# Later flips and value products in the first attention of a two-block transformer kernel

## The chip, the cores and the metric

One core of a Trainium2 chip runs the whole kernel in one launch. The metric is the device time of one execution in microseconds (us), as the median of several runs. Five engines with queues of their own work side by side: TensorE (PE, matmuls), VectorE (DVE), ScalarE (ACT), GpSimd (POOL) and SyncE (SP, which here issues the transfers).

## The reference

Two blocks run one after the other on 256 tokens with 2048 channels, all in float32. The change touches only the first stage, the attention of the first block:

```python
h = rms_norm(x, mixer_norm)                       # x is (1, 256, 2048)
q, k, v = split(h @ w_qkv)                        # 32 query heads, 4 key and value heads of 64
q, k = apply_rope(rms_norm(q, q_norm)), apply_rope(rms_norm(k, k_norm))
scores = q @ k.T / 8                              # in a band of 128 keys back; blocks of 128 queries
m = max(max(scores), sink)
probs = exp(scores - m) / (sum(exp(scores - m)) + exp(sink - m))
x = x + (probs @ v) @ w_o
```

The 32 query heads fall into 4 groups of 8, one for each key head. Behind this attention come a gated feed-forward, a mixer with a gated linear attention and a pooling branch, a cross attention and a second feed-forward, which the change leaves as they are.

## The kernel before, in words

**The large products.** Every projection is a product of activations (2 tiles `t` of 128 tokens) with a weight matrix that streams from memory in units of 512 rows by 512 columns. A unit is four k-tiles of 128 rows. To keep float32 accuracy, each number is split into a high and a low part, and a k-tile takes three matmuls for each `t` (`mm`, L280 to L282), six in all, into two PSUM banks tagged `acc`. The weights are split into `wh` (on ACT, L235) and `wl` (on DVE, L236), two k-tiles at a time and three such parts ahead.

**The first attention.** `attention` runs five chunks of 16 k-tiles through `gemm`: first the keys and values (k-tiles 0 to 15), then the query groups g = 0 to 3 (k-tiles 16 to 31, 32 to 47, 48 to 63, 64 to 79). Then the output projection `w_o` follows (from k-tile 80). In this text the k-tiles are numbered so, and "at k-tile n" means behind the six matmuls of k-tile n.

**Jobs.** What must be done with a finished chunk is a Python generator, a job. `gemm` calls `tick` after each k-tile, which counts every job's wait down by one; a job whose count is 0 writes its next instructions into the program, up to its next `yield n`, and comes up again n k-tiles later. TensorE takes its instructions in exactly the order in which the program writes them. The instructions of DVE, ACT and POOL are put in order by a scheduler that may move them; each of these engines then also works its list off in order. `norm_rope` writes its instructions with a raised priority. Where a later stage needs the output of a job that isn't finished, `need` runs the rest of the job at once.

**`kv_job`** starts 4 k-tiles after its chunk. It scales the values, normalises and rotates the keys (`norm_rope`: L611 on ACT, L613, L614, the power L445 on POOL, then L619, L621, L625, L627 and L630 on DVE), waits, and flips the keys with TensorE transposes (L663), one `t` per k-tile.

**`attn_job(g)`** starts when the chunk of its group is done. Group 0 rotates both `t` in one step, the other groups the first at once and the second 2 k-tiles later. Then, with waits between: flips of the queries (L681, four transposes for each `t`, copied by ACT L682), the scores of `t` = 0 (L695, 16 matmuls), the first half of the scores of `t` = 1 (8 matmuls), the flips of the probabilities of `t` = 0 (L725, twice four, copied by ACT L727), the second half of the scores of `t` = 1, the value products of `t` = 0 (L734, 16 matmuls into the one bank tagged `po`), the four flips of `t` = 1 with the value products of the flip before in the same k-tile (8 matmuls each), and two k-tiles later the flips of the output (L421), which become activations for `w_o`. Behind the scores, DVE adds the mask while it empties the bank (L700), takes the maximum (L702, L703), and ACT takes the exponentials (L708). L739 on DVE empties `po`, and the next value products wait for it. All small products of the jobs take turns in three PSUM banks tagged `aux`, and the temporaries in 12 buffers tagged `s2`.

The jobs of neighbouring groups overlap: that of group g is in its second half while the chunk of group g + 1 ends and that group's rotations begin.

Of the kernel before, what the change touches and what calls it, by code (L numbers as in the profile page):

```python
# [83 lines left out]
class _Net:  # L84
# [563 lines left out]
    def kv_job(self, kv):  # L648
        nc = self.nc
        yield 4  # L650
        self.need(self.start)
        v = self.s2([128, 2, 256])
        kd = [self.s2([128, 4, 2, 64]) for _ in range(2)]
        for t in range(2):
            nc.scalar.activation(v[:, t], kv[t][:, 256:512], AF.Identity, bias=0.0, scale=self.r[:, t:t + 1])
        self.norm_rope([z[:, 0:256].rearrange("p (h d) -> p h d", d=64) for z in kv], 4, (0, 1),
                       self.rope[1], 1.0, [[z[:, :, j] for j in range(2)] for z in kd])
        yield 9
        kT = self.s4([128, 4, 256])
        for t in range(2):  # L660
            b = self.bank((128, 4, 128))
            for h in range(4):
                nc.tensor.transpose(b[:, h], kd[t][:, h], self.ident)  # L663
            nc.scalar.copy(kT[:, :, t * 128:t * 128 + 128], b)
            yield 1
        return kT, v

    def attn_job(self, g, qs):

        nc = self.nc  # L670
        q = [self.s2([128, 4, 2, 64]) for _ in range(2)]
        for ts in ((0, 1),) if g == 0 else ((0,), (1,)):
            self.norm_rope([qs[t].rearrange("p (h d) -> p h d", d=64) for t in ts], 8, ts, self.rope[0], 0.125,
                           [[q[t][:, :, i] for i in range(2)] for t in ts], split=True)
            yield 7 if g == 0 else 4 if ts[0] else 3
        kT, v = self.need(self.kv)
        qT = self.s4([128, 4, 256])
        for t in range(2):
            b = self.bank((128, 4, 128))
            for j in range(4):  # L680
                nc.tensor.transpose(b[:, j], q[t][:, j], self.ident)  # L681
            nc.scalar.copy(qT[:, :, t * 128:t * 128 + 128], b)  # L682
            yield 2
        nm = [self.sm([128, 8]) for _ in range(2)]
        den = [self.sm([128, 8]) for _ in range(2)]

        def scores(t, u):

            nb, hp, res = t + 1, 4 // (t + 1), []
            mask = self.mask2 if t else self.mask1  # L690
            bs = [self.bank((128, hp, nb * 128)) for _ in range(2)]
            for i in range(hp):
                for half, b in enumerate(bs):
                    rows = slice(64 * half, 64 * half + 64)
                    nc.tensor.matmul(b[:, i], qT[rows, u + i, t * 128:t * 128 + 128],  # L695
                                     kT[rows, g, 0:nb * 128], start=True, stop=True)
            for half, b in enumerate(bs):
                h0 = 4 * half + u
                s = self.s2([128, hp, nb * 128])
                nc.vector.tensor_tensor(s, b, mask.unsqueeze(1).to_broadcast([128, hp, nb * 128]), op=ALU.add)  # L700
                mx = self.sm([128, hp])
                nc.vector.tensor_reduce(mx, s, axis=AX.X, op=ALU.max)  # L702
                nc.vector.scalar_tensor_tensor(nm[t][:, h0:h0 + hp], mx, -1.0,  # L703
                                               self.nsink[:, 8 * g + h0:8 * g + h0 + hp],
                                               op0=ALU.mult, op1=ALU.min)
                for i in range(hp):
                    h = h0 + i
                    nc.scalar.activation(s[:, i], s[:, i], AF.Exp, bias=nm[t][:, h:h + 1],  # L708
                                         accum_out=den[t][:, h:h + 1])
                res.append((h0, s))  # L710
            return res

        def totals(t):
            es = self.sm([128, 8])
            nc.vector.tensor_add(es, nm[t], self.sink[:, 8 * g:8 * g + 8])
            nc.scalar.activation(es, es, AF.Exp)
            nc.vector.tensor_add(den[t], den[t], es)
            nc.vector.reciprocal(den[t], den[t])

        def flipped(t, s):  # L720
            nb, hp = t + 1, 4 // (t + 1)
            b = self.bank((128, hp, nb, 128))
            for i in range(hp):
                for j in range(nb):
                    nc.tensor.transpose(b[:, i, j], s[:, i, j * 128:j * 128 + 128], self.ident)  # L725
            pt = self.s2([128, hp, nb, 128])
            nc.scalar.copy(pt, b)  # L727
            return pt

        def weighted(po, t, h0, pt):  # L730
            nb, hp = t + 1, 4 // (t + 1)
            for i in range(hp):
                for j in range(nb):
                    nc.tensor.matmul(po[:, h0 + i], pt[:, i, j], v[:, j, g * 64:g * 64 + 64],  # L734
                                     start=j == 0, stop=j == nb - 1)

        def rows(po, t):
            o = self.s2([128, 512])
            nc.vector.tensor_tensor(o.rearrange("p (h d) -> p h d", d=64), po,  # L739
                                    den[t].unsqueeze(2).to_broadcast([128, 8, 64]), op=ALU.mult)  # L740
            return o

        s0 = scores(0, 0)
        totals(0)
        yield 2
        s1 = scores(1, 0)
        yield 2
        p0 = [(h0, flipped(0, s0[0][1])) for h0 in (s0[0][0],)]
        yield 1
        p0.append((s0[1][0], flipped(0, s0[1][1])))  # L750
        yield 1
        s1 += scores(1, 2)
        totals(1)
        yield 1
        po = self.bank((128, 8, 64), "po")
        for h0, pt in p0:
            weighted(po, 0, h0, pt)
        o = [rows(po, 0)]
        yield 1
        po, prev = None, None  # L760
        for h0, s in s1:
            pt = flipped(1, s)
            yield 1
            if prev is not None:
                if po is None:
                    po = self.bank((128, 8, 64), "po")
                weighted(po, 1, *prev)
            prev = (h0, pt)
        yield 1
        weighted(po, 1, *prev)  # L770
        o.append(rows(po, 1))
        hl = yield from self.group_job(o, wait=2)
        return hl
# [558 lines left out]
```

## Time and profile before

| | |
|---|---|
| runs | 2686.42, 2686.44, 2686.57 us (median 2686.44) |
| profiled execution, its own time | 2686.66 us |
| its span, first to last instruction | 2684.5 us |
| PE busy | 2657.9 us (99%) |
| PEld (weight loads) busy | 2195.2 us (82%) |
| DVE busy | 1890.7 us (70%) |
| ACT busy | 1424.2 us (53%) |
| POOL busy | 27.1 us (1%) |
| DMA share of 16 engines | 51.4% |
| granted TensorE clock | 0.999 |

Busy is the union of an engine's instructions. A matmul of 512 columns is listed with 0.39 us, though the next one starts 0.23 us after it: they overlap, so a busy TensorE can still lose time. Idle time in the tables is that of the engine just before an instruction, with what ended it.

### The profile page before, as it was taken

The page shows a single profiled execution, that of the slowest core. Times are in us where ns is not written, and L with a number is a line of the kernel's source. Part 1 is how long each engine was busy: PE and PEld are TensorE (multiplying, and loading weights), DVE is VectorE, ACT ScalarE, POOL GpSimd, SP SyncE. Part 2 cuts the span into 40 slices and gives each one's busy share as a digit, 9 for nine tenths or more (in the row PEclk, how much of TensorE's full clock was granted, in tenths as well). Part 3 has the DMA queues.
Part 4 walks back from the last instruction along what each step waited for, and adds up shares of the span by engine and source line. Part 5 has one row for each costly group of instructions (what it writes and reads, how often), then busy time and mean ns, then how long its engine had stood idle before and what let it go on. Part 6 is the DMA issues. An engine that isn't in the chain of part 4 may idle for free.

```text
span 2684.5 us, 31592 instructions
## 1 busy us (share of the span) xinstructions
PE 2657.9 (99%) x12352; PEld 2195.2 (82%) x12352; DVE 1890.7 (70%) x2225; ACT 1424.2 (53%) x1849; POOL 27.1 (1%) x27
## 2 busy tenths in 40 slices
PE   8999999999999999999999999999999999999998
PEld 7778888888888888888888888888878888888887
DVE  7775799888888864655545555454578877777776
ACT  6555555555555555454444555444555655555554
POOL 0100000000000000000000000000000000000000
PEclk9999999999999999999999999999999999999999
DMA  7334455555555554445555566444554555555553
GB/s 304 113 126 145 169 218 187 205 192 206 209 195 200 194 187 178 151 172 188 188 190 193 183 225 212 172 157 168 183 180 175 190 193 194 192 190 195 194 193 138
DMA packets 74086, 499.61 MB, mean 186 GB/s; under 512 B 8496, under 2 KB 9392, under 8 KB 14928
## 3 DMA queue, kind: packets, MB, share of 16 engines
q1 hardware_dynamic: 73936, 497.59, 51.4%
q8 instruction: 97, 1.59, 0.2%
q14 instruction: 53, 0.43, 0.0%
HBM read 495.46 MB, written 2.10 MB: 185 GB/s over the span
## 4 chain that ended last, share of the span: by engine, by line
PE 97%; DVE 2%; ACT 1%; POOL 0%; DMA 0%; issue 0%; SPq 0%; POOLq 0%; DVEq 0%; ACTq 0%
PE acc L280 29%; PE acc L282 29%; PE acc L281 29%; PE aux L421 2%; PE aux L282 1%; PE aux L281 1%; PE aux L280 1%; PE po L734 1%; PE po L282 1%; PE po L281 1%; PE po L280 1%; PE aux L969 0%; POOL sm L445 0%; DVE wl L236 0%; DMA raw<-in_w_qkv 0%; PE aux L695 0%
## 5 line engine op out<-in xcount | busy, mean ns | idle before, releaser
L236 DVE TENSOR_TENSOR wl<-raw,wh 128x1024 fp32r<-128x1024 f32 (+1 forms) x1012 | 1230.7, 1220 | 689.0 <-ACT wh L235 677.1
L235 ACT CAST wh<-raw 128x1024 fp32r<-128x1024 f32 (+1 forms) x1012 | 1060.2, 1051 | 1084.0 <-PE acc L282 1020.6
L280 PE MATMUL acc<-wh,s 128*128 128x512 f32 x3440 | 1364.1, 397 | 7.4 <-ACT wh L235 5.5
L282 PE MATMUL acc<-wh,s 128*128 128x512 f32 x3440 | 1342.6, 390 | 0.6 <-DVE s L404 0.6
L281 PE MATMUL acc<-wl,s 128*128 128x512 f32 x3440 | 1341.0, 390 | 0.4 <-DVE wl L236 0.4
L280 PEld LDWEIGHTS acc<-wh,s 128*128 128x128 f32 x3440 | 646.9, 188 | 145.5 <-DVE s L382 7.1
L282 PEld LDWEIGHTS acc<-wh,s 128*128 128x128 f32 x3440 | 646.2, 188 | 138.1 <-DVE s L404 1.1
L281 PEld LDWEIGHTS acc<-wl,s 128*128 128x128 f32 x3440 | 647.3, 188 | 128.2 <-DVE wl L236 1.7
L467 DVE TENSOR_TENSOR x<-acc,x 128x512 f32<-128x512 f32 x112 | 72.8, 682 | 0.0
L421 PEld LDWEIGHTS aux<-con,s 128*128 128x128 f32 x408 | 50.2, 140 | 15.7 <-issue 4.0
L421 PE MATMUL aux<-con,s 128*128 128x128 f32 x408 | 60.9, 272 | 1.8 <-DVE s L1162 1.8
L1159 ACT ACTIVATE s<-aux,vec 128x256 f32<-128x256 f32 x88 | 47.9, 560 | 12.5 <-PE aux L421 7.8
L403 ACT CAST s<-aux 128x512 fp32r<-128x512 f32 x66 | 38.4, 584 | 28.9 <-PE aux L421 18.6
L445 POOL TENSOR_TENSOR sm<-sm,mhalf 128x2 f32<-128x2 f32 (+3 forms) x22 | 26.0, 1182 | 2651.0 <-DVE sm L453 2314.1
L404 DVE TENSOR_TENSOR s<-aux,s 128x512 fp32r<-128x512 f32 x66 | 44.6, 687 | 11.5 <-ACT s L403 10.3
L408 ACT ACTIVATE s<-aux,vec 128x256 fp32r<-128x256 f32 x80 | 37.7, 473 | 22.3 <-PE aux L421 14.2
L280 PE MATMUL aux<-wh,s 128*128 128x512 f32 x120 | 46.7, 389 | 0.0
L281 PE MATMUL aux<-wl,s 128*128 128x512 f32 x120 | 46.7, 389 | 0.0
L282 PE MATMUL aux<-wh,s 128*128 128x512 f32 x120 | 46.7, 389 | 0.0
L409 DVE SCALAR_TENSOR_TENSOR s<-aux,vec,s 128x256 fp32r<-128x256 f32 x80 | 38.3, 482 | 6.5 <-ACT s L408 5.3
L1160 DVE SCALAR_TENSOR_TENSOR s<-aux,vec,s 128x255 f32<-128x255 f32 x88 | 41.0, 478 | 2.4 <-ACT s L1159 0.2
L1162 DVE SCALAR_TENSOR_TENSOR s<-aux,vec,s 128x254 f32<-128x254 f32 x88 | 40.0, 477 | 1.1
(195 smaller groups left out, 1309.1 us busy)
## 6 DMA issues: line engine op xcount, KB each, us to landing
raw<-in_w_up SPq DMA_DIRECT2D x132, 1024.0 KB, 4.8
raw<-in_w_dn SPq DMA_DIRECT2D x88, 1024.0 KB, 4.8
raw<-in_w_in SPq DMA_DIRECT2D x64, 1024.0 KB, 4.8
raw<-in_w_gate SPq DMA_DIRECT2D x44, 1024.0 KB, 4.8
raw<-in_w_ckv SPq DMA_DIRECT2D x32, 1024.0 KB, 4.7
raw<-in_w_qkv SPq DMA_DIRECT2D x19, 1024.0 KB, 5.4
raw<-in_w_o SPq DMA_DIRECT2D x16, 1024.0 KB, 4.7
raw<-in_w_br SPq DMA_DIRECT2D x16, 1024.0 KB, 4.7
```

Of the source, the lines that this page charges most:

```text
L235: nc.scalar.copy(h[:, m], raw[:, m])
L236: nc.vector.tensor_sub(l[:, m], raw[:, m], h[:, m].bitcast(F32))
L280: nc.tensor.matmul(o, ah[:, k, s], h, start=first, stop=False)
L281: nc.tensor.matmul(o, ah[:, k, s], l, start=False, stop=False)
L282: nc.tensor.matmul(o, al[:, k, s], h, start=False, stop=last)
L403: nc.scalar.copy(h[:, k0:k0 + n], src)
L404: nc.vector.tensor_sub(l[:, k0:k0 + n], src, h[:, k0:k0 + n].bitcast(F32))
L421: self.nc.tensor.transpose(b[:, j, t * 128:t * 128 + 128], srcs[t][:, (k + j) * 128:(k + j) * 128 + 128], self.ident)
L467: nc.vector.tensor_add(xs[t], pss[t], xs[t])
L1159: nc.scalar.activation(y[:, j], b[:, j], AF.Identity, bias=bb, scale=w2)
L1160: nc.vector.scalar_tensor_tensor(y[:, j, 1:256], b[:, j, 0:255], w1, y[:, j, 1:256], op0=ALU.mult, op1=ALU.add)
L1162: nc.vector.scalar_tensor_tensor(y[:, j, 2:256], b[:, j, 0:254], w0, y[:, j, 2:256], op0=ALU.mult, op1=ALU.add)
```

## The change

Five waits of the jobs become longer; no instruction is added or taken away. The keys are flipped 10 k-tiles after their rotation was written instead of 9. In group 0 the first query flips come 9 k-tiles after the rotation instead of 7. In groups 0 to 2 the first flip of the probabilities of `t` = 0 comes 3 k-tiles after the scores instead of 2, and the value products of `t` = 0 come 2 k-tiles after the second half of the scores of `t` = 1 instead of 1. All that a job does behind a longer wait moves with it; group 3 keeps its waits.

```diff
@@ kv_job
                        self.rope[1], 1.0, [[z[:, :, j] for j in range(2)] for z in kd])
-        yield 9
+        yield 10
         kT = self.s4([128, 4, 256])
@@ attn_job
             self.norm_rope([qs[t].rearrange("p (h d) -> p h d", d=64) for t in ts], 8, ts, self.rope[0], 0.125,
                            [[q[t][:, :, i] for i in range(2)] for t in ts], split=True)
-            yield 7 if g == 0 else 4 if ts[0] else 3
+            yield 9 if g == 0 else 4 if ts[0] else 3
         kT, v = self.need(self.kv)
...
         s1 = scores(1, 0)
-        yield 2
+        yield 3 if g < 3 else 2
         p0 = [(h0, flipped(0, s0[0][1])) for h0 in (s0[0][0],)]
         yield 1
         p0.append((s0[1][0], flipped(0, s0[1][1])))
         yield 1
         s1 += scores(1, 2)
         totals(1)
-        yield 1
+        yield 2 if g < 3 else 1
         po = self.bank((128, 8, 64), "po")
```

The places in k-tiles, before and after, worked out from the waits:

| | group 0 | group 1 | group 2 |
|---|---|---|---|
| rotations written | 31 (both) | 47 and 49 | 63 and 65 |
| query flips | 37, 39 → 39, 41 | 53, 55 | 69, 71 |
| scores of t = 0, first half of t = 1 | 41, 43 → 43, 45 | 57, 59 | 73, 75 |
| flips of t = 0 | 45, 46 → 48, 49 | 61, 62 → 62, 63 | 77, 78 → 78, 79 |
| second half of the scores of t = 1 | 47 → 50 | 63 → 64 | 79 → 80 |
| value products of t = 0 | 48 → 52 | 64 → 66 | 80 → 82 |
| flips of t = 1 | 49 to 52 → 53 to 56 | 65 to 68 → 67 to 70 | 81 to 84 → 83 to 86 |
| value products of t = 1 | 51 to 54 → 55 to 58 | 67 to 70 → 69 to 72 | 83 to 86 → 85 to 88 |
| output flips | 56, 57 → 60, 61 | 72, 73 → 74, 75 | 88, 89 → 90, 91 |

Group 3 rotates at 79 and 81, flips its queries at 85 and 87, and goes on as the groups before it did. The flips of the keys move from k-tiles 27 and 28 to 28 and 29.

## Rows read from the trace of the kernel before

**Rows 1.** The page's section 1, all engines: busy us (share) xinstructions.
```profile
PE 2657.9 (99%) x12352; PEld 2195.2 (82%) x12352; DVE 1890.7 (70%) x2225; ACT 1424.2 (53%) x1849; POOL 27.1 (1%) x27
```

**Rows 2.** The page's section 5, high part of the weights: | busy, mean ns | idle before, releaser.
```profile
L235 ACT CAST wh<-raw 128x1024 fp32r<-128x1024 f32 (+1 forms) x1012 | 1060.2, 1051 | 1084.0 <-PE acc L282 1020.6
```

**Rows 3.** Waits of PE, whole span: waited for, total us, times, longest.
```profile
PE aux L725 <- DVE s L700: 3.5, 3, 1.4
PE aux L681 <- DVE s L630: 2.8, 2, 1.6
...
PE po L734 <- DVE sm L703: 1.4, 3, 0.5
```

**Rows 4.** Timeline of PE, group 0's query flips: start, us, instructions, [idle before].
```profile
58.83 0.39 PE L280 MATMUL acc<-wh,s 128*128 128x512 f32 x1
...
62.68 0.39 PE L282 MATMUL acc<-wh,s 128*128 128x512 f32 x1
64.22 0.66 PE L681 MATMUL aux<-con,s 128*128 128x128 f32 x4 [1.15 <-DVE s L630]
...
67.25 0.39 PE L282 MATMUL acc<-wh,s 128*128 128x512 f32 x1
69.25 0.63 PE L681 MATMUL aux<-con,s 128*128 128x128 f32 x4 [1.61 <-DVE s L630]
```

**Rows 5.** Timeline of PE, group 0 beside group 1's rotations.
```profile
89.98 0.60 PE L725 MATMUL aux<-con,s 128*128 128x128 f32 x4
...
99.78 0.61 PE L725 MATMUL aux<-con,s 128*128 128x128 f32 x4
```

**Rows 6.** Timeline of PE, group 1 beside group 2's rotations.
```profile
122.44 1.13 PE L695 MATMUL aux<-s,s 64*128 64x256 f32 x8
124.98 1.89 PE L734 MATMUL po<-s,s 128*128 128x64 f32 x16
128.15 0.60 PE L725 MATMUL aux<-con,s 128*128 128x128 f32 x4
131.22 0.63 PE L725 MATMUL aux<-con,s 128*128 128x128 f32 x4 [1.07 <-DVE s L700]
133.67 1.08 PE L734 MATMUL po<-s,s 128*128 128x64 f32 x8 [0.44 <-DVE sm L703]
...
137.54 0.61 PE L725 MATMUL aux<-con,s 128*128 128x128 f32 x4
```

**Rows 7.** Timeline of PE, group 3, which has no rotations beside it.
```profile
203.75 0.60 PE L725 MATMUL aux<-con,s 128*128 128x128 f32 x4
205.58 0.60 PE L725 MATMUL aux<-con,s 128*128 128x128 f32 x4
...
210.91 0.61 PE L725 MATMUL aux<-con,s 128*128 128x128 f32 x4
```

**Rows 8.** Timeline of DVE, the last rotations of group 0.
```profile
63.40 0.76 DVE L630 TENSOR_TENSOR s<-s,s 128x256 f32<-128x256 f32 x2
...
68.35 0.75 DVE L630 TENSOR_TENSOR s<-s,s 128x256 f32<-128x256 f32 x2
```

**Rows 9.** Timeline of DVE, group 1 beside group 2's rotations.
```profile
129.71 0.76 DVE L630 TENSOR_TENSOR s<-s,s 128x256 f32<-128x256 f32 x2
130.39 1.28 DVE L700 TENSOR_TENSOR s<-aux,con 128x512 f32<-128x512 f32 x2
...
132.84 0.69 DVE L739 TENSOR_TENSOR s<-po,sm 128x512 f32<-128x512 f32 x1
...
134.72 0.68 DVE L613 TENSOR_REDUCE sm<-s 128x8 f32<-128x512 f32 x1
...
141.01 0.76 DVE L630 TENSOR_TENSOR s<-s,s 128x256 f32<-128x256 f32 x2
```

**Rows 10.** Timeline of POOL, the powers of group 2's two rotations.
```profile
124.61 2.56 POOL L445 TENSOR_TENSOR sm<-sm,mhalf 128x8 f32<-128x8 f32 x1 [24.99 <-DVE sm L614]
135.75 1.64 POOL L445 TENSOR_TENSOR sm<-sm,mhalf 128x8 f32<-128x8 f32 x1 [8.58 <-DVE sm L614]
```

## The prediction

> **What bounds the kernel now.** The first view to read is the busy time by engine: TensorE is busy for 2657.9 of 2684.5 us, so a change can give back only TensorE's waits or what they hide [rows 1]. The costliest groups come next: ACT sits idle for 1084.0 us ahead of the high parts of the weights, and 1020.6 of that ends with a matmul that frees a weight buffer [rows 2]. The weights wait for TensorE, not TensorE for the weights, so time saved on TensorE is kept until something else is late.
>
> Then TensorE's own waits. Three of the longest entries belong to the jobs of the first attention: flips of `t` = 1 that wait for the mask additions (3.5 us, three times), query flips that wait for the last step of the rotation (2.8 us, twice) and value products that wait for DVE (1.4 us, three times) [rows 3]. Together 7.7 us in 2684. All other changes of the time must come through these eight waits or through new ones.
>
> What do they cost with the overlap that a stopped TensorE loses? Group 3 has the same flips with no rotation beside it and serves as the measure. Its four flips of `t` = 1 take 7.16 us from the start of the first to that of the last [rows 7]. Beside group 1's rotations they take 9.80 us [rows 5], beside group 2's 9.39 us [rows 6]; the place beside group 3's rotations shows the same two waits as the latter, to 0.01 us, and counts as it. That is 2.64, 2.23 and 2.23 us. The query flips of group 0 start 1.54 and 2.00 us after the last matmul ahead of them began, where matmuls follow each other every 0.23 us: 3.08 us [rows 4]. All in all 10.18 us can be won here, no more.
>
> **Part 1: the flips of keys and queries of group 0.** Nothing is added: the same four transposes, copies and scores run two k-tiles later, the key flips one. A k-tile without small work takes 1.36 us (58.83 to 62.68 and the 0.23 us of its last matmul are three of them) [rows 4]. In the new order TensorE doesn't stop at 62.91 but runs two more k-tiles and comes to the first flip at 65.6. The rotated queries are ready at 64.2 (63.40 and 0.76) [rows 8]: no wait. From the first flip to TensorE's coming to the second there are 3.26 us (64.22 to 67.25 and 0.23) [rows 4], so it comes there at 68.9. The second half is ready at 69.1 (68.35 and 0.75) [rows 8] and the flip began 0.15 after that: a wait of 0.35 stays. Gain 2.73. Its two bounds are 3.08 and 1.6 (should the second rotation end 1.1 later, as much as the first flip waited). The key flips have no entry among the waits: zero, hidden by the same products.
>
> **Part 2: the second half of the job, groups 1 and 2.** Why does the flip wait? At k-tile 63 the job of group 2 writes its first rotation, then the job of group 1 its scores. DVE works off the rotation first, to 130.4, and only then the masks that empty the banks, from 130.39 on, then the output rows, which empty `po`, until 133.5 (132.84 and 0.69). The second rotation follows and ends at 141.8 [rows 9]. I count from T = 122.4, the end of the products of k-tile 63 [rows 6]: masks begin at T+8.0, the first bank is empty at T+8.6, the second at T+9.2, `po` at T+11.1, the second rotation is done at T+19.3.
>
> Now TensorE in the new order. A flip with the k-tile behind it takes 1.83 us [rows 7], scores with theirs 2.54, sixteen value products with theirs 3.17 [rows 6], eight value products with flip and k-tile 2.67 (205.58 to 210.91, two of them) [rows 7], so the eight alone 0.84. At k-tile 63 stands now a flip, then: scores of k-tile 64 at T+1.8, end of 65 at T+4.4, value products of 66 at T+5.8, first flip of `t` = 1 at T+9.0, the second at T+10.8, the next value products at T+12.6. The second flip finds its bank empty for 2.2 us, and the value products find `po` empty for 1.5 us. Both waits go. What is late next is the second query flip of group 2 at k-tile 71, which the change does not move: 12.6 + 2.67 + 0.4 for the first query flip + 2.67 + 0.84 = T+19.2 against a rotation that ends at T+19.3. I charge 0.1 us. Gain 2.13 at each of the two places, 4.26 together. This holds if DVE keeps its order (rotation, masks, output rows, second rotation). Its order is not written by the kernel: the scores now come one k-tile later and the value products two, while the second rotation stays, so it may come ahead of them. The bounds are 2.23 and, with it ahead, a loss of 3.5 each (below).
>
> **Part 3: group 0 beside group 1's rotations.** Here the scores move from k-tile 47 to 50, behind both rotations (47, 49), and all else by four. With U as the end of the products of k-tile 47: two flips with k-tiles, then the scores at U+5.1, the value products at U+9.0, flips at U+12.2 and U+14.4, value products at U+16.2. If DVE does the second rotation first, it has up to 5.4 us more before the masks: from 134.72 to 141.77 are 7.05 us, with 1.64 of the power on POOL [rows 9, 10], which can hide under the first rotation. Then the masks begin at U+13.4, the bank is empty at U+14.0 (in time), and `po` 3.1 us after the masks began (2.45 to the output rows, 0.69 for them), at U+16.5: a wait of 0.3. With POOL's time not hidden everything is 1.6 later, 2.15 us with the lost overlap. Gain between 0.5 and 2.64; I take 2.0, nearer to the hidden case, as the flips come so much later.
>
> **Sum.** 2.73 + 4.26 + 2.0 = 9.0 us. The profiled execution has 2686.66 us in all, 2.16 around its span; minus 9.0 this is 2677.7. The median of the runs lies 0.22 below it: 2677.4, the forecast. The DMA issues on SP are the same and run with the weight parts; nothing waits on POOL's queue but the powers.
>
> A rule speaks against part 2. The two powers of group 2's rotations, alike in shape, took 2.56 and 1.64 us [rows 10], so something can hold one up by 0.92 us. The Trainium skill (SBUF — State Buffer, section "SBUF: two separate sides") says that a VectorE instruction with two SBUF inputs and a GpSimd instruction that reads SBUF share a port pair, and that the one that starts second waits for the whole of the first. The two durations agree with it; by the rule every power that the new order puts behind such a DVE instruction would take the longer time, and by the row of the short one none of group 2's second powers would.
>
> **The rivals.**
>
> *The second power is held up* (chance 0.10). If the second power takes 2.56 instead of 1.64 us, the second rotation ends 0.92 later, and the unmoved query flip of k-tiles 71 and 87 waits 1.0 instead of 0.1. Gain 7.2, time 2679.2. For it: the long power exists; against it: the short one has stood at this place. The page that would make it so is the one named above.
>
> *DVE turns round* (0.30). The second rotation is written at k-tile 65 with raised priority, before too little DVE work is left to be done first. In group 1 and 2 the masks then begin 5.4 us later, at T+13.4. The flip comes at T+10.8 and waits for T+14.0, 3.2 us; the value products come at T+15.8 and wait for `po` at T+16.5, 0.7 us. With 0.2 of lost overlap that is 4.1 instead of 2.23 at each place: 1.9 lost twice, against 2.73 and 2.3 won: 1.3 us, time 2685.2. For it: scores and output rows move, the rotation doesn't. Against it: before, the output rows went ahead of the second rotation, though they had been written only one k-tile earlier [rows 9].
>
> *The same in full, slower* (0.08). The second rotation keeps POOL's time and its weight splits, all 7.05 us, and masks begin at T+15.0. Waits of 4.85 and 0.7 with 0.2 lost: 5.75 instead of 2.23, 3.5 lost twice; part 3 keeps 0.5. 2.73 + 0.5 - 7.0 = -3.8 us, time 2690.2. It decides from masks that begin 5.5 us later than now: there the two places eat what parts 1 and 3 give.
>
> *The waits move along* (0.07). Only part 1 does what it says; behind it the DVE work that ends the waits comes later by as much as TensorE does, since both are written by the same job. Gain 2.7, time 2683.7. Against it: masks wait for the rotation now, not for the scores [rows 9].
>
> **How the numbers follow.** The forecast has the remaining 0.45, with its own range from 2676.3 (all 10.18 won) to 2680.1 (parts 1 and 3 at their lower bounds, 1.6 and 0.5). To leave no more than 2 in 10 out, the range must reach the case of 2685.2: 2676.2 to 2685.5. A measurement of this kernel tells about 0.2%, 5.4 us, from no change, so faster means below 2681.1: the forecast, the held power, and a little of the mixed cases, 0.56. Slower would need over 2691.8, beyond the slower rival's own sum: 0.03. Same: 0.41.
>
> **What would show it.** Part 1: in TensorE's waits the entry of query flips on the rotation falls from two to one of about 0.35 us. Part 2: the flip's entry on the masks goes, the one on `po` too, and a new short one of a query flip may appear around k-tiles 71 and 87; in DVE's timeline the masks stand ahead of the second rotation's first reduction. If they stand behind it, the second rival holds. Part 3: four flips of group 0 take 7.2 to 7.5 us. The forecast is wrong if TensorE's waits on masks or output rows keep over 2 us in sum.

## The result, and the profile after

The changed kernel takes 2705.04 us (median of 6 runs, 2703.63 to 2707.05), the kernel before 2686.69 in the same runs (2686.42 to 2688.02). The ratio is 1.0068, with a 95% interval of 1.0055 to 1.0081: it is 18 us slower, where 9 us less were forecast. Its profiled execution took 2703.63 us, with a span of 2701.8.

The page's busy times, engine by engine, hardly differ from those of before [rows 1], though the span is 17.3 us longer:

```profile
PE 2662.5 (99%) x12352; PEld 2201.8 (81%) x12352; DVE 1890.9 (70%) x2225; ACT 1425.1 (53%) x1849; POOL 26.0 (1%) x27
```

TensorE's waits show where the time went. These are the entries of the jobs in the kernel after (waited for, total us, times, longest); the flips' and value products' entries of [rows 3] are gone:

```profile
PE po L734 <- DVE s L739: 14.5, 2, 7.4
...
PE aux L681 <- DVE s L700: 4.2, 1, 4.2
...
PE aux L681 <- DVE s L630: 0.2, 1, 0.2
```

Together 18.9 us instead of 7.7. Two waits of 7.1 and 7.4 us are for the single bank `po`, one of 4.2 us is for an `aux` bank. TensorE's timeline (start, us, instructions, [idle before]) shows first group 0's query flips, which answer to [rows 4], then the 4.2 us, then group 1 beside group 2's rotations, which answers to [rows 6]:

```profile
66.09 0.60 PE L681 MATMUL aux<-con,s 128*128 128x128 f32 x4
...
69.07 0.39 PE L282 MATMUL acc<-wh,s 128*128 128x512 f32 x1
69.70 0.63 PE L681 MATMUL aux<-con,s 128*128 128x128 f32 x4 [0.24 <-DVE s L630]
...
98.42 1.08 PE L681 MATMUL aux<-con,s 128*128 128x128 f32 x4 [4.18 <-DVE s L700]
...
101.62 0.60 PE L725 MATMUL aux<-con,s 128*128 128x128 f32 x4
...
125.11 1.13 PE L695 MATMUL aux<-s,s 64*128 64x256 f32 x8
129.07 1.89 PE L734 MATMUL po<-s,s 128*128 128x64 f32 x16
...
132.25 0.60 PE L725 MATMUL aux<-con,s 128*128 128x128 f32 x4
...
134.08 0.60 PE L725 MATMUL aux<-con,s 128*128 128x128 f32 x4
...
135.68 0.40 PE L282 MATMUL acc<-wh,s 128*128 128x512 f32 x1
143.20 1.94 PE L734 MATMUL po<-s,s 128*128 128x64 f32 x8 [7.12 <-DVE s L739]
...
147.50 0.63 PE L282 MATMUL acc<-wh,s 128*128 128x512 f32 x1
147.92 0.63 PE L280 MATMUL acc<-wh,s 128*128 128x512 f32 x1
...
149.17 1.00 PE L734 MATMUL po<-s,s 128*128 128x64 f32 x8
...
150.91 0.39 PE L282 MATMUL acc<-wh,s 128*128 128x512 f32 x1
151.14 0.39 PE L280 MATMUL acc<-wh,s 128*128 128x512 f32 x1
```

At 132.25 and 134.08 the two flips of `t` = 1 go through without a wait, as forecast. Then the value products of `t` = 1 stand for 7.12 us. VectorE's timeline says why; its first two lines are the place beside group 1, the others the place of [rows 9]:

```profile
96.92 0.76 DVE L630 TENSOR_TENSOR s<-s,s 128x256 f32<-128x256 f32 x2
97.59 1.28 DVE L700 TENSOR_TENSOR s<-aux,con 128x512 f32<-128x512 f32 x2
...
130.03 0.76 DVE L630 TENSOR_TENSOR s<-s,s 128x256 f32<-128x256 f32 x2
130.71 1.28 DVE L700 TENSOR_TENSOR s<-aux,con 128x512 f32<-128x512 f32 x2
...
134.57 0.68 DVE L613 TENSOR_REDUCE sm<-s 128x8 f32<-128x512 f32 x1
...
141.69 0.76 DVE L630 TENSOR_TENSOR s<-s,s 128x256 f32<-128x256 f32 x2
142.37 0.69 DVE L739 TENSOR_TENSOR s<-po,sm 128x512 f32<-128x512 f32 x1
```

The masks (L700) still come before the second rotation, but the output rows (L739), which empty `po`, now come behind all of it: at 142.37, where before they began at 132.84, ahead of the rotation's 134.72 [rows 9]. Beside group 1 the masks too stand behind the second rotation, at 97.59.

Behind these waits TensorE also runs slower for a while. At 147.50 the products follow each other every 0.42 us, at 150.91 every 0.23 us. In the kernel before they keep 0.23 us behind the longest wait of these stages, 1.61 us, too (eight from 69.94 to 71.54), and the granted clock of 91 to 102, 129 to 153 and 176 to 198 us is 1.00 there. In the kernel after (us, PE busy and instructions, PEclk, DMA share, GB/s):

```profile
91.00:102.00 11.00, 6.82 (x38) 0.84 0.29 95
102.00:129.00 27.00, 27.00 (x167) 1.00 0.33 118
129.00:153.00 24.00, 16.88 (x96) 0.79 0.25 88
153.00:176.00 23.00, 23.00 (x136) 1.00 0.26 92
176.00:198.00 22.00, 14.58 (x82) 0.84 0.29 96
```

1.00 is the level of 2.4 GHz; 0.79 and 0.84 are means over stretches that are partly at 1.2 GHz. The three lower stretches are those of the three long waits. From the start of k-tile 36 to that of k-tile 104, which holds all moved work of groups 0 to 2, TensorE took 158.93 us before and 175.35 after: 16.4 of the 17.0 us by which the profiled executions differ.

### The profile page after: what moved, and what is told of

Same layout as the page of the kernel before. It is cut to its first block, busy times and chain, and to the rows that moved or that the text cites. A ratio compares the mean times of both kernels' runs of the same rounds, so it can differ in the third digit from the quotient of the medians.

```text
span 2701.8 us, 31591 instructions
## 1 busy us (share of the span) xinstructions
PE 2662.5 (99%) x12352; PEld 2201.8 (81%) x12352; DVE 1890.9 (70%) x2225; ACT 1425.1 (53%) x1849; POOL 26.0 (1%) x27
## 4 chain that ended last, share of the span: by engine, by line
PE 95%; DVE 2%; ACT 1%; POOL 0%; issue 0%; DMA 0%; SPq 0%; POOLq 0%; DVEq 0%; ACTq 0%
PE acc L280 29%; PE acc L282 28%; PE acc L281 28%; PE aux L421 2%; PE aux L282 1%; PE aux L281 1%; PE aux L280 1%; PE po L734 1%; DVE wl L236 1%; PE po L282 1%; PE po L281 1%; PE po L280 1%; POOL sm L445 0%; PE aux L969 0%; ACT s L708 0%
## 5 line engine op out<-in xcount | busy, mean ns | idle before, releaser
L236 DVE TENSOR_TENSOR wl<-raw,wh 128x1024 fp32r<-128x1024 f32 (+1 forms) x1012 | 1230.9, 1221 | 706.0 <-ACT wh L235 694.3
L404 DVE TENSOR_TENSOR s<-aux,s 128x512 fp32r<-128x512 f32 x66 | 44.7, 687 | 10.7 <-ACT s L403 9.4
```

The lines of the kernel that those rows point to most:

```text
L236: nc.vector.tensor_sub(l[:, m], raw[:, m], h[:, m].bitcast(F32))
L404: nc.vector.tensor_sub(l[:, k0:k0 + n], src, h[:, k0:k0 + n].bitcast(F32))
```

## The experiments

**The theories, a letter each in the expectations.** A: the output rows have slipped behind the second rotation in VectorE's list, and behind both rotations stand group 0's masks; nothing is wrong with TensorE's own new places. B: the new places on TensorE are themselves at fault (small work in other company, banks taken in another sequence), and VectorE's list is a symptom. The first expectations also name C: the lower clock has a reason of its own, and the waits are a minor part. A further one, D, came out of the first runs: a copy on ScalarE (L727) is late because exponentials stand ahead of it.

**Second rotations two k-tiles later than in the changed kernel.** A rotation holds no TensorE instruction, so TensorE's list is that of the changed kernel.

```diff
-            yield 9 if g == 0 else 4 if ts[0] else 3
+            yield 9 if g == 0 else 2 if ts[0] else 5
```

> The changed kernel with one thing moved: in groups 1 to 3 the second rotation is written two k-tiles later (at k-tiles 51, 67, 83 instead of 49, 65, 81). TensorE's program is the same as in the changed kernel, instruction by instruction; only the order of VectorE's and ScalarE's work differs: beside groups 2 and 3 the output rows that empty po now stand ahead of the second rotation, beside group 1 they still stand behind it. Theory A (the time is lost where the value products wait for output rows queued behind the second rotation): the two waits of 7.1 and 7.4 us on po go, and with them the slow clock after them; beside group 1 a wait of about 4 us comes in place of the 4.2 us there. Some 2680 to 2686 us. Theory B (the small products simply come too late in TensorE's program and push the work behind them together, whatever VectorE's order): nothing changes, 2703 to 2707. Theory C (the lower granted clock is there for a reason of its own, the waits are a minor part): the waits go but the clock stays at 0.995, about 2690 to 2695.

Measured: 2689.39 us, ratio to before 1.0007 (0.9998 to 1.0016). That is 3.4 us over A's range and close under C's, so the trace has to decide. VectorE beside group 2's rotations:

```profile
131.12 1.28 DVE L700 TENSOR_TENSOR s<-aux,con 128x512 f32<-128x512 f32 x2
...
133.58 0.68 DVE L739 TENSOR_TENSOR s<-po,sm 128x512 f32<-128x512 f32 x1
...
136.86 0.69 DVE L613 TENSOR_REDUCE sm<-s 128x8 f32<-128x512 f32 x1 [0.55 <-ACT s L611]
...
144.07 0.76 DVE L630 TENSOR_TENSOR s<-s,s 128x256 f32<-128x256 f32 x2
```

The output rows are ahead of the rotation again, and both long waits are gone: some 15 us of the 18 come back with TensorE's list untouched. The lower clock goes with the waits: it is 1.00 from 129 to 153 us and from 168 to 192, and lower only around the wait beside group 1 (0.88 from 91 to 102, 0.79 from 102 to 112). A holds, B and C fall. The rest of the miss has two waits: beside group 1 the output rows are still behind the rotation (4.3 us, once), and the query flips, which stay where they were, wait for the later rotation (3.0 us in three waits, 1.4 the longest).

**Second rotations earlier, in the kernel before.** The counterpart: the kernel before with the rotation written at k-tiles 47, 63 and 79, ahead of the value products. TensorE's list is that of before.

```diff
-            yield 7 if g == 0 else 4 if ts[0] else 3
+            yield 7 if g == 0 else 6 if ts[0] else 1
```

> The kernel before with one thing moved: the second rotation of groups 1 to 3 is written two k-tiles earlier (47, 63, 79 instead of 49, 65, 81). TensorE's program is that of the kernel before, instruction by instruction; on VectorE the output rows now stand behind the second rotation, as in the changed kernel. Theory A: value products wait for po at all three places, 5 to 9 us each, in place of waits of 0.4 to 0.5; 2702 to 2712 us. Theory B (lateness in TensorE's program): no change, 2686. Theory C: time and clock as before, 2686 to 2690.

Measured: 2718.89 us, ratio 1.0116 (1.0101 to 1.0131), longer than expected. TensorE's wait and, beside group 2's rotations, VectorE:

```profile
PE po L734 <- DVE s L739: 26.0, 3, 8.7
```

```profile
141.75 1.28 DVE L700 TENSOR_TENSOR s<-aux,con 128x512 f32<-128x512 f32 x2
...
145.61 0.68 DVE L613 TENSOR_REDUCE sm<-s 128x8 f32<-128x512 f32 x1
...
151.72 0.76 DVE L630 TENSOR_TENSOR s<-s,s 128x256 f32<-128x256 f32 x2
152.40 0.68 DVE L739 TENSOR_TENSOR s<-po,sm 128x512 f32<-128x512 f32 x1
```

With none of the change's edits the same sequence gives the same wait, at three places. So the place of the rotation makes the loss, with TensorE's list untouched. My size was too small: the waits are up to 8.7 us long, and the granted clock of the stretches around them is 0.74 to 0.83 (95 to 115, 140 to 162 and 185 to 215 us).

**The first two edits alone** (keys, queries of group 0).

```diff
-        yield 9
+        yield 10
...
-            yield 7 if g == 0 else 4 if ts[0] else 3
+            yield 9 if g == 0 else 4 if ts[0] else 3
```

> The first two edits alone: keys flipped after 10 k-tiles, queries of group 0 after 9. The small products of group 0 all come two k-tiles later, those of groups 1 to 3 where they were. VectorE's order beside group 1: rotation, masks, second rotation, output rows; beside groups 2 and 3 as before. Theory A: 2.7 us won at the query flips, and one wait of about 7 us on po (with a us or two of slow clock) beside group 1 in place of 2.6 us lost there; 2688 to 2692 us. Theory B: the shift by two k-tiles alone wins 2.7 to 5 us, 2681 to 2684.

Measured: 2692.73 us, ratio 1.0019 (1.0010 to 1.0028). The query flips' wait goes, but group 0's later half now meets group 1's second rotation at k-tile 49: its output rows fall behind it, and the value products wait 5.3 us once. So not even part 1 can be had by itself.

**The third edit alone** (flips of the probabilities of `t` = 0 one k-tile later).

```diff
-        yield 2
+        yield 3 if g < 3 else 2
         p0 = [(h0, flipped(0, s0[0][1])) for h0 in (s0[0][0],)]
```

> The third edit alone: in groups 0 to 2 the flips of the probabilities of t = 0 and all behind them come one k-tile later. VectorE keeps rotation, masks, output rows, second rotation at all three places. Theory A: the second flip's wait on the masks and the one on po go at all three places, up to 2.6 + 2.2 + 2.2 us; the query flips of group 0 still wait; 2679 to 2682 us. Theory B: lateness costs by the k-tile, 2690 or more. Theory C: no change of the clock, 2680 to 2686.

Measured: 2692.79 us, ratio 1.0018 (1.0009 to 1.0028). I had expected a gain. The time is one that B gave, but the waits show another cause: those for masks and for VectorE's maximum go, yet value products wait for L727, 7.8 us in four waits. TensorE and ScalarE beside group 2's rotations:

```profile
136.90 0.60 PE L725 MATMUL aux<-con,s 128*128 128x128 f32 x4
...
140.84 1.10 PE L734 MATMUL po<-s,s 128*128 128x64 f32 x8 [1.95 <-ACT s L727]
```

```profile
137.19 0.51 ACT L708 ACTIVATE s<-s,sm 128x256 f32<-128x256 f32 x1 [3.50 <-DVE sm L703]
...
139.28 1.03 ACT L235 CAST wh<-raw 128x1024 fp32r<-128x1024 f32 x1
140.21 1.05 ACT L727 COPY s<-aux 128x512 f32<-128x512 f32 x2
```

The copy of a flip that was ready at 137.5 starts at 140.21: it stands in ScalarE's list behind the exponentials, which wait 3.50 us for VectorE's maximum, and behind the weight cast that follows them. That is theory D.

**The fourth edit alone** (value products of `t` = 0 one k-tile later).

```diff
-        yield 1
+        yield 2 if g < 3 else 1
         po = self.bank((128, 8, 64), "po")
```

> The fourth edit alone: the value products of t = 0 come 2 k-tiles after the second half of the scores of t = 1, in groups 0 to 2. VectorE keeps rotation, masks, output rows, second rotation at all three places, as the second rotation is still the later by enough. Theory A: no long wait on po, so it isn't this edit by itself that costs 18 us but its sum with the others that moves the output rows past the second rotation; within 6 us of the kernel before. If the fourth edit did it by itself, 12 us slower or more. Theory D: the waits on masks go and come back as waits of 2 to 3 us on copies behind the exponentials, 2 to 6 us slower.

Measured: 2695.99 us, ratio 1.0032 (1.0020 to 1.0043), 8.7 us slower, more than A or D said. No wait for output rows; the copies again, and one wait of 1.1 us for masks:

```profile
PE po L734 <- ACT s L727: 8.9, 3, 3.2
```

**The first three edits, without the fourth.**

```diff
-        yield 2 if g < 3 else 1
+        yield 1
         po = self.bank((128, 8, 64), "po")
```

> The changed kernel without its fourth edit: the value products of t = 0 come one k-tile after the scores again. Beside groups 2 and 3 VectorE keeps rotation, masks, output rows, second rotation; beside group 1 both rotations stand ahead of the masks. Theory A: the waits on po of 7 us go, some 15 us faster than the changed kernel. Theory D: in their place value products wait about 2 us at each of two places for copies on ScalarE, and some 5 us beside group 1 on masks, so about 0 to 4 us slower than the kernel before. If the fourth edit isn't what does the harm, it stays at 2703 or more.

Measured: 2689.96 us, ratio 1.0010 (1.0000 to 1.0019). The `po` waits go; 4.6 us for L727 in three waits stay, and 4.2 us for masks at one flip (L725). So the 7 us waits need the third and fourth edits together: one k-tile each lets the value products be written at 65, in the same step as the rotation and ahead of it, and only both put them at 66. The first two edits, the third and the fourth lose 4.7, 4.7 and 8.7 us by themselves, together as much as the whole change. That is chance: the first three together lose 2.5, and the waits of the parts are others than those of the whole.

**The whole change, with rotations written late enough.** Against the changed kernel. The second rotations are written at k-tiles 52, 67 and 83: at each of the three places in the same k-tile as the value products of `t` = 0 or behind it.

```diff
-            yield 9 if g == 0 else 4 if ts[0] else 3
+            yield 9 if g == 0 else ((6, 2), (5, 3), (5, 2))[g - 1][ts[0]]
```

> The changed kernel with the second rotations written late enough that VectorE keeps rotation, masks, output rows, second rotation at all three places (waits of the two rotations: 6 and 2 k-tiles in group 1, 5 and 3 in group 2, 5 and 2 in group 3); the query flips of groups 1 and 2 come one k-tile later, as a look at the second rotation's end in the first run asks for. Theory A (output rows behind the second rotation are the whole loss): no wait on po above 0.5 us and none on the masks; 4 to 8 us faster than the kernel before. Theory D (the time saved on the masks is lost in ScalarE's queue, where the copies of the flips stand behind the exponentials, as in the run of the third edit alone): value products wait 1 to 3 us for those copies, and it is within 2 us of the kernel before.

Measured: 2684.31 us, ratio 0.9990 (0.9981 to 1.0000), 3.2 us less than before: less than A said, more than D. No wait for masks or output rows is left. New ones: scores (L695) on the copy L727 (2.1 us in two waits) and on L404, the low part of an output flip (1.0 us), and three query flips of 0.8 us in all. From k-tile 36 to 104 it takes 156.06 us, 2.9 less than before.

**The same without the first two edits.** Against the kernel before; the rotations stand at 51, 67 and 83.

```diff
-            yield 7 if g == 0 else 4 if ts[0] else 3
+            yield 7 if g == 0 else ((5, 3), (5, 3), (5, 2))[g - 1][ts[0]]
...
-        yield 2
+        yield 3 if g < 3 else 2
...
-        yield 1
+        yield 2 if g < 3 else 1
```

> The third and fourth edit without the first two (keys after 9, queries of group 0 after 7), and with the second rotations late enough that VectorE keeps its order (waits 5 and 3, 5 and 3, 5 and 2). Theory A: the query flips of group 0 wait 2.8 us as before, nothing waits for masks or po; 3 to 6 us faster than the kernel before. Theory D: 1 to 3 us of waits on the copies at each place; within 2 us of the kernel before.

Measured: 2689.98 us, ratio 1.0008 (0.9999 to 1.0018). With VectorE's sequence right, the third and fourth edits gain nothing that can be measured: TensorE's waits at the jobs are 3.0, 2.1, 1.9 and 1.0 us, 8.0 in all against 7.7 before. Of the 4.9 us that parts 2 and 3 take from the masks and maxima, 4.0 come back as waits for ScalarE's copies and 1.0 as one for L404.

**Group 0's later half left short.** Third and fourth edit for groups 1 and 2 only, rotations to suit.

```diff
-            yield 9 if g == 0 else 4 if ts[0] else 3
+            yield 9 if g == 0 else ((5, 2), (4, 3), (4, 3))[g - 1][ts[0]]
...
-        yield 3 if g < 3 else 2
+        yield 3 if 0 < g < 3 else 2
...
-        yield 2 if g < 3 else 1
+        yield 2 if 0 < g < 3 else 1
```

> All four edits, but the third and fourth only in groups 1 and 2, with the second rotation waits 5 and 2 in group 1, 4 and 3 in groups 2 and 3; VectorE keeps its order at all three places. Theory A: no wait on po above 0.5 us; 2 to 6 us faster than the kernel before. Theory D: beside group 1, where scores and value products stand as close as before, value products wait 2 to 4 us for copies behind the exponentials; no more than 2 us faster.

Measured: 2687.04 us, ratio 0.9999 (0.9990 to 1.0008). 4.6 us of waits for L727 in three, 1.1 at the scores. No gain, as D said.

**TensorE kept busy during the wait.** The changed kernel with 60 transposes ahead of the value products of `t` = 1 in groups 1 and 2, into a bank that nobody reads. They are meant to lie in the wait and to change only what TensorE does there.

```diff
+            if g in (1, 2):
+                fill = self.bank((128, 4, 128))
+                for i in range(60):
+                    nc.tensor.transpose(fill[:, i % 4], self.ident, self.ident)
             po = self.bank((128, 8, 64), "po")
```

> The changed kernel with 60 transposes of the identity into a bank of their own ahead of the first value products of t = 1 in groups 1 and 2, where TensorE waits 7.1 and 7.4 us: work of about 5.5 us that nobody reads, in time that was idle. If the lower granted clock behind the long waits costs time of its own (k-tiles there took 12.06 and 3.87 us, where wait and work alone make 10.2 and 2.7): the clock stays nearer to 1 and the run is 3 to 6 us faster than the changed kernel, 2699 to 2702. If the clock costs nothing, it is the same as the changed kernel or slower by what of the filling doesn't fit, 2704 to 2708.

Measured: 2699.65 us, ratio 1.0046 (1.0029 to 1.0063); the interval overlaps that of the changed kernel, so the trace has to decide. TensorE there, and the two stretches' granted clock:

```profile
135.91 0.40 PE L282 MATMUL acc<-wh,s 128*128 128x512 f32 x1
136.15 6.71 PE L769 MATMUL aux<-con 128*128 128x128 f32 x60
143.45 1.08 PE L734 MATMUL po<-s,s 128*128 128x64 f32 x8 [0.59 <-DVE s L739]
...
146.63 1.00 PE L734 MATMUL po<-s,s 128*128 128x64 f32 x8
```

```profile
129.00:153.00 24.00, 23.41 (x172) 1.00 0.26 89
176.00:198.00 22.00, 21.11 (x155) 1.00 0.27 96
```

The wait is as long as without the filling: 7.54 us from the last product to the value products, 7.52 in the changed kernel. But from there to the next value products TensorE needs 3.18 us instead of 5.97 (143.20 to 149.17). At the other place it is 3.19 instead of 5.17. The lower clock behind the two waits costs 2.8 and 2.0 us, and it comes from TensorE's standing still. In the third lower stretch, where nothing was filled in, it stays (0.71 from 91 to 102 us).

**Output flips one k-tile earlier.** All in order, as above, and the output flips of groups 1 and 2 moved away from the next group's scores.

```diff
-        hl = yield from self.group_job(o, wait=2)
+        hl = yield from self.group_job(o, wait=1 if 0 < g < 3 else 2)
```

> The kernel with all four edits and VectorE's order kept at all three places, and in groups 1 and 2 the output flips one k-tile earlier (1 k-tile after the last rows instead of 2), so that they don't stand in one k-tile with the first scores of t = 1. Theory A (VectorE's order is what counts): as the run with the order kept, 2 to 4 us faster than the kernel before, and 1 us better yet if the wait of 1.0 us of scores on the low part of an output flip goes. Theory E (what is left is a shortage of the three banks, which any shift only moves): the 1 us comes back at another wait, same as the run with the order kept.

Measured: 2682.78 us, ratio 0.9984 (0.9975 to 0.9993). The wait for L404 is gone; these are left:

```profile
PE aux L695 <- ACT s L727: 2.1, 2, 1.0
...
PE aux L681 <- DVE s L630: 1.0, 3, 0.4
```

It beats both kernels, by 4.5 us the one before and by some 22 the changed one. Whether the last edit adds to it is open: it ran beside other runs of before than the kernel without it, their intervals overlap, and k-tiles 36 to 104 take 156.30 us against 156.06. The two traces differ in one more thing. This one has a stretch at the lower clock behind a wait of only 1.05 us, the other has 1.00 there (118 to 134 us; 0.89 here):

```profile
124.34 1.13 PE L695 MATMUL aux<-s,s 64*128 64x256 f32 x6 [1.05 <-ACT s L727]
...
126.63 0.63 PE L280 MATMUL acc<-wh,s 128*128 128x512 f32 x1
127.06 0.63 PE L281 MATMUL acc<-wl,s 128*128 128x512 f32 x1
```

The products come every 0.42 us until 129.15. By their spacing that costs some 1.6 us (an estimate), which may hide a gain of the last edit.

## Why the prediction was wrong

**Part 1 was right.** The second query flip waits 0.24 us (0.35 forecast) and the first not at all. By the prediction's own measure the two now lose 0.40 us (69.07 to 69.70, less 0.23) instead of 3.08: a gain of 2.68 for 2.73. What it left out is that the edit also moves group 0's output rows behind a rotation, 5.3 us when it is made alone.

**Part 2 failed in its condition, "this holds if DVE keeps its order (rotation, masks, output rows, second rotation)".** Up to there its count was good. With T = 123.3 (scores at 125.11, T+1.8), the masks begin at T+7.4 (8.0 forecast), and TensorE is at the value products at T+12.6 (12.6 forecast: 135.68 and 0.23). But `po` is empty at T+19.8 (142.37 and 0.69) instead of T+11.1: 8.7 us late. The prediction added that this order "is not written by the kernel", and let a doubt stand in for a look. The table of places answers it: second rotation at 65; before, scores at 63 and value products at 64; after, scores at 64 and value products at 66. The masks stay ahead and the output rows pass behind. The sign that it gave for this part, masks ahead of the second rotation, came true (130.71 against 134.57) and proved nothing, since it left out the output rows; its sum of waits over 2 us, here 18.7, told the failure. In the timelines of all thirteen kernels, at three places in each, VectorE takes masks, output rows and second rotations in the sequence in which the jobs write them; within one k-tile the older job comes first. The scheduler's own rule isn't shown by that, but the sequence was there to be read.

**The rivals moved the wrong thing.** "DVE turns round" and "the same in full, slower" put the masks behind the rotation and let the output rows follow 3.1 us later. None moved the output rows alone. So the bound of "3.5 each" was wrong in kind and size: the waits are 7.1 and 7.4 us, since TensorE comes to `po` early and the whole rotation stands ahead of it, 7.88 us here (134.57 to 142.45) where before it took 7.05.

**The clock was no term of the sum.** In the kernel before the products kept their 0.23 us behind stops of up to 1.6 us, and I took a wait to cost its length and a little overlap. Behind the long ones TensorE ran on at its lower level: 2.8 and 2.0 us, and 1.4 us behind the 4.18 us (98.42 to 101.62 is 3.20, a flip with its k-tile 1.83 [rows 7]); only the first two were tested.

**Part 3 was mis-sized.** The masks do come behind both rotations, as it assumed. Its price was 0.3 to 2.15 us at `po` or a flip. What came is one wait of 4.18 us, of the next group's query flip for an `aux` bank that the masks had still to empty. The three banks go round among all jobs; the part counted only its own two. By its own figures that query flip, directly behind the first flip, came at U+12.6 to a bank that was empty at U+14.0: 1.4 us that it left out. The rest is that the masks came late, at U+16.6 (97.59; U = 81.0) instead of U+13.4: the first rotation ended 1.7 us later than assumed, and the second took 7.06 us (90.62 to 97.68) with the power's time not hidden. The four flips of group 0 take 13.75 us (93.65 to 107.40), where 7.2 to 7.5 were the sign.

**ScalarE's list was not weighed at all.** The runs with the sequence put right say that parts 2 and 3 wouldn't have held even then. They gain nothing alone (1.0008), where 6.3 us were forecast, mainly because copies stand behind exponentials that wait for VectorE. With all four edits and the sequence put right, 3.2 us of the 9.0 are gained, and 4.5 with the output flips moved as well. "The waits move along" was the rival nearest to that, with another mechanism.

**The rival of the second power** was right in its mechanism. GpSimd's powers of the two rotations of group 2 [rows 10] in the kernel after:

```profile
124.85 1.64 POOL L445 TENSOR_TENSOR sm<-sm,mhalf 128x8 f32<-128x8 f32 x1 [31.49 <-DVE sm L614]
135.59 2.54 POOL L445 TENSOR_TENSOR sm<-sm,mhalf 128x8 f32<-128x8 f32 x1 [9.11 <-DVE sm L614]
```

The long and the short time have changed places. The 0.90 us are part of the 7.12, as VectorE waits for this power. The Trainium skill's rule (SBUF — State Buffer, section "SBUF: two separate sides"), that of a VectorE instruction with two SBUF inputs and a GpSimd instruction that reads SBUF the one that starts second waits for the whole of the first, agrees: in VectorE's timeline a split (L236, 1.22 us, two SBUF inputs) begins at 135.42, ahead of the power that took 2.54, and none runs at the start of the one that took 1.64.

**The balance** of the 16.4 us in k-tiles 36 to 104: 11.2 from the waits (18.9 less 7.7), 6.1 from the lower clock (2.8, 2.0, 1.4), less the 2.5 that the old waits lost in overlap (10.18 less 7.7). That is 14.8. The new waits lose some overlap too, 0.15 to 0.17 us each by the measure of the old ones, 0.65 in all; about 1 us is not assigned. Open too is why the best version wins 4.5 us of the 10.18 that I took for winnable, though its waits have fallen to 3.1.

## What to carry to other kernels

Where several jobs share an engine that works its list off in order, moving one job's work also moves what frees its buffers past the other jobs' work: for every place, list what each in-order engine, VectorE and ScalarE alike, then has ahead of the release of a bank, the single ones first. A forecast that ends with "if the order stays" isn't done until the places in the program have been compared. And a stall of several microseconds on TensorE should be priced at its length and the slower stretch behind it, 1.4 to 2.8 us here.

## What the runs showed of the hardware

TensorE's clock fell inside a kernel that keeps it busy for 99% of the span: behind 7.1 to 7.4 us of standing still it ran at its lower level (products every 0.42 us) until some 4 to 6 us later, 149.2 in the first case. With 60 transposes of no use in the wait the granted clock of the same stretch was 1.00.

The length of a wait alone doesn't tell whether a slower stretch follows, nor how long it is. Behind 1.05 us (124.34, the last run) and 1.91 us (100.81, the third and fourth edits in order) products came every 0.42 us for a while; behind 1.91 us (137.24, without the fourth edit) and 2.18 us (135.60, group 0 left short) they kept 0.23. Behind the same wait of 4.2 us the spacing was back at 0.23 us 3.0 us after its end in the changed kernel (101.39) and 4.7 us after it in the run with the transposes (102.55). Why is not shown.

The page's busy share says little of all this: 99% before and after. The lost time in which TensorE stood still is a small part of the span, and a product at the lower level is listed with a longer time (0.63 us, 0.39 at the higher) and counts as busy.
